# Value projections of four heads in one matmul, and an earlier first quad, in a two-layer encoder trunk

## The chip, the cores and the metric

The kernel runs on one core of a Trainium2 chip. The metric is device time in microseconds (us), the median of several executions of the same program. Beside it stands one execution taken with the hardware profiler, whose rows are quoted here. Its span is the time from the first to the last instruction on the core; the device time of the same execution is a little longer than the span.

Engine names in the profile: PE is TensorE (matmuls), PEld its weight loads, DVE is VectorE, ACT is ScalarE, POOL is GpSimd, and SP issues most of the DMAs. Each engine works through its own instructions in a fixed order; semaphores let one engine wait for another. PSUM, which matmuls write, has eight banks of 128 partitions by 512 fp32 values.

## What is computed

The reference is a streaming encoder trunk on one sequence of 512 tokens, width 1024, two layers, all in fp32. Each layer is:

```python
h = h + 0.5 * swiglu(rmsnorm(h, ffn1_norm), ffn1_w_gu, ffn1_w_down)        # width 2816
u = rmsnorm(h, mix_norm)
b_g, c_g, v_c, q_c, kv_c, k_r, g_conv, g_mla = split(u @ w_in)
y_conv = (b_g * causal_conv3(c_g * v_c)) @ w_conv_out
y_mla = mla(q_c, kv_c, k_r) @ w_mla_out                                     # 8 heads
h = h + (sigmoid(g_conv) * y_conv + sigmoid(g_mla) * y_mla) @ w_o
h = h + 0.5 * swiglu(rmsnorm(h, ffn2_norm), ffn2_w_gu, ffn2_w_down)
h = h + sigmoid(rmsnorm(h, ple_norm) @ w_ple_gate) * (p @ w_ple_proj)
```

The attention (mla) has eight heads with a key and query part of 128 columns, a rotary part of 64 and a value of 128. Keys and values come from a normed latent of width 256 (kv_c), queries from one of width 384 (q_c). The mask lets a token see its own chunk of 64 tokens and all chunks before. A final RMSNorm follows the last layer.

## The kernel before

**Numbers as pairs.** To reach fp32 accuracy, every matmul operand is split into a high part rounded to fp32r and a low part, the rest. A product is three matmuls: high times high, high times low, low times high (`mm3`, L264 to L270). ACT makes a high part by a cast (L260), DVE the low part by a subtraction (L261). Most matmuls have 512 columns, one PSUM bank.

**Weights.** `Stream` brings weights in halves of eight 128x128 tiles (128x1024, 512 KB), in the order in which the kernel asks for tiles. A half is loaded into one of ten raw buffers (L52, queue SP), then split: a cast on ACT (L71, `wh`), a subtraction on DVE (L72, `wl`). There are four buffers for split halves (`N_WH`), and `get` hands out the tiles of the current half one after the other; a request must lie within one half. `fill` tells how many tiles of the current half are used up. During the attention three of the raw buffers hold the turned probabilities (`pt`).

**Buffers of activations.** 44 buffers of 128x512 (`G`) hold all that is not a weight; `gates` (16), the split latent `kvc` (4), keys, queries, values, exponentials and rotary parts share them in the attention.

**PSUM.** `Banks` has two layouts. `paired` has two double banks (`PB`), one double bank (`PA`, for sums that are seeded by a copy) and two single banks (`PS`). `eight` has eight single ones, used in turn; a tile waits until the last reader of the bank's earlier content is done.

**Order.** A planner that knows rough costs puts the instructions of each engine in order when the kernel is built; the earlier an instruction is written, the higher it ranks, but one that can't run yet lets later ones by. The order is then fixed. So the trace, not the source, tells the order on ACT and DVE; TensorE's order follows the source nearly everywhere.

**The first SwiGLU** (`ffn` with `first`, L661 on). Products with the gate and up weights run partly as plain matmuls (`projs`, four columns pairs 0 to 3) and partly as quads: a seven-product scheme over token halves (`Halved`, `Sevens`). A quad needs sums and differences of rows of the input. `Halved.row(j)` is `own(j)`, one multiplication on ACT and one difference on DVE, which give what products 1 and 5 need, and `other(j)`, all the rest, for products 2, 3, 4, 6 and 7. `step(n, 1)` does product 1 into a double bank `b` and has ACT copy it to the seeded double bank `a` (`seed`, L543); `step(n, 2)` goes on adding to `a`. `activate(f)` turns the plain products of column pair f into activations, and `down` multiplies these with the down weights.

**The attention** (`mixer`, from L845). Heads go in four pairs. For a pair, `keys_queries` does key 0, query 0, key 1, query 1 (two and three weight tiles each), `values` the values of both heads. Value weights are fetched by `value_weights` after both queries or between, whichever fits into halves of eight tiles. In `values` the split latent of 128 tokens is the stationary operand, and the weights of the two heads, 256 columns, are the moving one. Two token blocks fill one bank: 24 matmuls of 256 columns and two banks for each pair. `scores` (L925 on) does four score tiles per head, 256 to 512 columns, five matmuls each, and for each a reduction on DVE (L943) and an exponential on ACT (L945). `turn` transposes the probabilities (L955) and splits them into `pt`; `mix_v` multiplies them with the values (L966 to L968).

For pair 0 keys and queries are done in the `paired` layout: key 0 in the first half of `PA`, query 0 in `PB`, key 1 and query 1 in the single banks. Then come `banks.eight()`, the values of pair 0, the table load for the exponential (L987) and the last of eight `conv_out`. The round of pair `pr` does the keys and queries of the next pair with the turning of this pair's first head between, `mix_v` of head 0, the next pair's first scores, its values, the turning of head 1, the next pair's second scores, the rotary part of the pair after that, and `mix_v` of head 1.

Names in the trace: `m0h1v` is layer 0, pair 1, values; `kn`, `qn` and `qr` are keys, queries and rotary queries; `m0s11p` the scores of pair 1, head 1; `m0t01t` the turned tiles of pair 0, head 1; `m0cop` conv_out; `a02b` and `a02a` the double banks of quad 2 of the first SwiGLU.

Of the kernel before, what the change touches and what calls it, by code (L numbers as in the profile page):

```python
# [16 lines left out]
P = 128  # L17
CHUNK = 64
N_HEADS = 8
NOPE = 128  # L20
ROPE = 64
VD = 128
# [160 lines left out]
def trunk_kernel(ctx, tc, dims, x, p, positions, gains, rope_c, final_row, weights, out):  # L183
# [46 lines left out]
    def PS(name):  # L230
        return banks.single.tile([P, 512], F32, tag="mm", name=name)
# [47 lines left out]
    def projs(cols_, vs, pss, part_by_part=False):  # L279

        for k, (vh, vl) in enumerate(vs):
            ws = [W.get(tiles[k]) for tiles in cols_]
            if k == 0 and part_by_part:
                for ps, (wh, _) in zip(pss, ws):
                    nc.tensor.matmul(ps, wh, vh, start=True, stop=False)
                for ps, (_, wl) in zip(pss, ws):
                    nc.tensor.matmul(ps, wl, vh, start=False, stop=False)
                for ps, (wh, _) in zip(pss, ws):
                    nc.tensor.matmul(ps, wh, vl, start=False, stop=False)
                continue  # L290
# [288 lines left out]
    def ffn(l, nm, name, first=False, beside=iter(()), early=2):  # L579
# [85 lines left out]
        if first:  # L665
            pss[0], pss[1] = whole(0), whole(1)
            projs(cs[0] + cs[1], xs, pss[0] + pss[1], True)
            r = norm()
            ys.row(0, xs)
            ys.row(1, xs)  # L670
            activate(0)
            pss[2] = [PS(f"{name}p{w}2") for w in "gu"]
            projs(cs[2], xs, pss[2])
            ys.row(2, xs)
            activate(1)
            ys.row(3, xs)
            pss[3] = whole(3)
            projs(cs[3], xs, pss[3])
            activate(2)
            step(n0, 1)  # L680
            activate(3)
            downs.extend((m, 0) for m in range(KD))
            for j in (2, 6, 5, 7, 3):
                if j in (2, 6, 5):
                    fill()
                step(n0, j)
        else:
            pss[0] = whole(0)
# [12 lines left out]
            step(n0, 7)  # L701
            step(n0, 3)
# [32 lines left out]
    def mixer(l):  # L735
# [108 lines left out]
        class Pair:  # L844
            def __init__(self, pr):  # L845
                self.n = f"{name}h{pr}"
                self.heads = (2 * pr, 2 * pr + 1)
                self.turned, self.q2, self.kn, self.qn, self.v = None, {}, {}, {}, None

            def q_rope(self):  # L850
                ps = proj(W.col("w_uq", l, tuple(hd * (NOPE + ROPE) + NOPE for hd in self.heads), QL), qc, self.n + "qr")
# [14 lines left out]
                ps = proj(W.col("w_uq", l, self.heads[t] * (NOPE + ROPE), QL), qc, f"{self.n}qn{t}", ps)  # L866
                self.qn[t] = split(ps, f"{self.n}qn{t}")

            def value_weights(self):
                self.vw = [W.get(*(("w_ukv", l, k * P, hd * 256 + NOPE) for hd in self.heads)) for k in range(KL // P)]  # L870

            def values(self):
                vs = []
                for tb in range(0, NT, 2):
                    ps = PS(f"{self.n}v{tb}")
                    for b in range(2):
                        tok = slice((tb + b) * P, (tb + b + 1) * P)
                        o = ps[:, b * 256:(b + 1) * 256]
                        for k, (vh, vl) in enumerate(self.vw):
                            ch, cl = kvc[k][0][:, tok], kvc[k][1][:, tok]  # L880
                            nc.tensor.matmul(o, ch, vh, start=k == 0, stop=False)
                            nc.tensor.matmul(o, ch, vl, start=False, stop=False)
                            nc.tensor.matmul(o, cl, vh, start=False, stop=k == len(self.vw) - 1)
                    vs.append(ps)
                self.v = [split(ps, f"{self.n}v{2 * i}") for i, ps in enumerate(vs)]

            def keys_queries(self, turned=None, pss=(None, None)):

                last = W.pairs_fit(2, 10)
                for t in range(2):  # L890
                    self.key(t, None if t else pss[0])
                    if t:
                        self.q_parts()
                        if not last:
                            self.value_weights()
                    self.query(t, None if t else pss[1])
                    if t == 0 and turned:
                        turned()
                if last:
                    self.value_weights()  # L900

        pairs = [Pair(pr) for pr in range(N_HEADS // 2)]
        n_last = KD // 2 - 1
# [55 lines left out]
        def mix_v(pr, t, qk):  # L959
            n = f"{name}o{pr}{t}"  # L960
            ps = PS(n + "av")
            for j in range(NT):
                vh, vl = qk.v[j // 2]
                c = (j % 2) * 256 + t * VD
# [15 lines left out]
        pt_h, pt_l = turned_tiles(name)  # L980
        heads = []
        NP = N_HEADS // 2
        pairs[0].keys_queries(pss=(PA(name + "kn")[:, 0, :], PB(name + "qn")[:, 0, :]))
        banks.eight()
        pairs[0].values()

        nc.scalar.activation(warm, m_b[KD - 1][:, 0:1], AF.Exp)  # L987
        conv_out(KD - 1)
        es = [scores(0, 0, pairs[0])]
        pairs[1].q_rope()  # L990
        es.append(scores(0, 1, pairs[0]))
        for pr in range(NP):
            qk = pairs[pr]
            if pr + 1 < NP:
                nxt, es_n = pairs[pr + 1], []
                nxt.keys_queries(lambda: turn(pr, 0, es[0]))
                heads.append(mix_v(pr, 0, qk))
                es_n.append(scores(pr + 1, 0, nxt))
                nxt.values()
                turn(pr, 1, es[1])  # L1000
                es_n.append(scores(pr + 1, 1, nxt))
                if pr + 2 < NP:
                    pairs[pr + 2].q_rope()
                heads.append(mix_v(pr, 1, qk))
                es = es_n
            else:
                for t in range(2):
                    turn(pr, t, es[t])
                    mla_part(t, 0, N_HEADS - 2)
                    heads.append(mix_v(pr, t, qk))  # L1010
# [261 lines left out]
```

## Time and profile before

| | |
|---|---|
| device time, median of 3 (lowest to highest) | 2266.15 us (2266.03 to 2266.27) |
| device time of the profiled execution | 2266.17 us |
| its span | 2264.0 us |
| granted TensorE clock, mean | 0.999 |
| matmuls | 12176 |
| instructions on DVE, ACT | 2423, 2220 |
| read from memory | 218.94 MB, 98 GB/s over the span |
| DMA queue of the weights | 29.1% of 16 engines' time |

In the waits, "PE x <- DVE y: 1.6, 1, 1.6" is TensorE's instruction on x waiting for DVE's on y: total, times and longest, in us. In the timelines a row has start, duration, engine, line, operation, output and inputs, shape and count; square brackets give idle time before it and what ended it. Matmuls overlap, so the difference of two starts is what one costs. A row of the windows view has the stretch, its length, and the busy time and count of PE, PEld, DVE, ACT and POOL, then the granted clock, the DMA share and GB/s.

### The profile page before, as it was taken

The page shows a single profiled execution, that of the slowest core. Times are in us where ns is not written, and L with a number is a line of the kernel's source. Part 1 is how long each engine was busy: PE and PEld are TensorE (multiplying, and loading weights), DVE is VectorE, ACT ScalarE, POOL GpSimd, SP SyncE. Part 2 cuts the span into 40 slices and gives each one's busy share as a digit, 9 for nine tenths or more (in the row PEclk, how much of TensorE's full clock was granted, in tenths as well). Part 3 has the DMA queues.
Part 4 walks back from the last instruction along what each step waited for, and adds up shares of the span by engine and source line. Part 5 has one row for each costly group of instructions (what it writes and reads, how often), then busy time and mean ns, then how long its engine had stood idle before and what let it go on. Part 6 is the DMA issues. An engine that isn't in the chain of part 4 may idle for free.

```text
span 2264.0 us, 31169 instructions
## 1 busy us (share of the span) xinstructions
PE 2247.3 (99%) x12176; PEld 1953.1 (86%) x12176; DVE 1721.0 (76%) x2423; ACT 1432.2 (63%) x2220; POOL 40.3 (2%) x42
## 2 busy tenths in 40 slices
PE   9999999999999999999999999999999999999998
PEld 7888888888888888888888888888888888888887
DVE  8887767877876877776798777668878678777756
ACT  7666666556744666666676666655567457666664
POOL 0000000000200000000000000000001000000000
PEclk9999999999999999999999999999999999999999
DMA  5232333222122233333222333332222223233321
GB/s 215 98 105 101 112 121 102 70 99 95 50 99 85 85 102 103 103 112 132 83 94 97 102 108 105 112 103 80 98 75 65 103 75 103 97 108 104 111 93 38
DMA packets 63362, 223.04 MB, mean 99 GB/s; under 512 B 7280, under 2 KB 7280, under 8 KB 63216
## 3 DMA queue, kind: packets, MB, share of 16 engines
q1 hardware_dynamic: 62640, 220.28, 29.1%
q8 instruction: 95, 1.56, 0.3%
q10 hardware_dynamic: 576, 0.79, 0.1%
q14 instruction: 51, 0.42, 0.1%
HBM read 218.94 MB, written 2.10 MB: 98 GB/s over the span
## 4 chain that ended last, share of the span: by engine, by line
PE 98%; DVE 1%; ACT 1%; issue 0%; DMA 0%; SPq 0%; DVEq 0%; ACTq 0%
PE a1pd L268 2%; PE b1pd L268 2%; PE b0pd L268 2%; PE a0pd L268 2%; PE b1pd L269 2%; PE a1pd L269 2%; PE b0pd L269 2%; PE a1pd L270 2%; PE b0pd L270 2%; PE b1pd L270 2%; PE a0pd L269 2%; PE a0pd L270 2%; PE m0mop L268 1%; PE m1mop L269 1%; PE m0mop L269 1%; PE m1mop L270 1%
## 5 line engine op out<-in xcount | busy, mean ns | idle before, releaser
L72 DVE TENSOR_TENSOR wl<-st,wh 128x1024 fp32r<-128x1024 f32 (+1 forms) x504 | 610.3, 1213 | 322.2 <-ACT wh L71 321.3
L71 ACT CAST wh<-st 128x1024 fp32r<-128x1024 f32 (+1 forms) x503 | 523.7, 1044 | 420.9 <-issue 13.6
L152 DVE TENSOR_TENSOR st<-st,st 128x1024 f32<-128x1024 f32 x47 | 57.5, 1224 | 1.3
L72 DVE TENSOR_TENSOR wl<-s,wh 128x1024 fp32r<-128x1024 f32 x47 | 57.3, 1219 | 0.6 <-ACT wh L71 0.4
L154 DVE TENSOR_TENSOR s<-st,st 128x1024 f32<-128x1024 f32 x47 | 57.3, 1219 | 0.2
L149 DVE TENSOR_TENSOR st<-st,s 128x1024 f32<-128x1024 f32 x47 | 57.3, 1218 | 0.0
L157 DVE TENSOR_TENSOR st<-st,st 128x1024 f32<-128x1024 f32 x47 | 57.2, 1217 | 0.0
L71 ACT CAST wh<-s 128x1024 fp32r<-128x1024 f32 x47 | 49.0, 1042 | 8.8 <-PE a1p L269 2.6
L632 ACT ACTIVATE h<-a0pd 128x512 f32<-128x512 f32 x40 | 23.7, 596 | 17.7 <-PE a0pd L270 17.5
L632 ACT ACTIVATE h<-b1pd 128x512 f32<-128x512 f32 x40 | 23.7, 596 | 16.8 <-PE b1pd L270 16.7
L632 ACT ACTIVATE h<-b0pd 128x512 f32<-128x512 f32 x40 | 23.7, 596 | 16.8 <-PE b0pd L270 16.6
L632 ACT ACTIVATE h<-a1pd 128x512 f32<-128x512 f32 x40 | 23.7, 596 | 16.4 <-PE a1pd L270 16.3
L628 ACT ACTIVATE a0pd<-h 128x512 f32<-128x512 f32 x40 | 24.0, 602 | 2.5 <-DVE a010o L548 1.7
L628 ACT ACTIVATE b1pd<-h 128x512 f32<-128x512 f32 x40 | 24.0, 603 | 2.2 <-DVE b110o L548 1.4
L628 ACT ACTIVATE a1pd<-h 128x512 f32<-128x512 f32 x40 | 24.0, 602 | 2.2 <-DVE a110o L548 1.4
L628 ACT ACTIVATE b0pd<-h 128x512 f32<-128x512 f32 x40 | 24.0, 603 | 2.2 <-DVE b010o L548 1.4
L107 POOL MEMSET wh<- 128x256 f32 x4 | 1.1, 314 | 1180.0 <-DVE wl L72 1180.0
L270 PE MATMUL a0p<-a0x,wl 128*128 128x512 f32 x44 | 17.1, 389 | 0.0
L268 PE MATMUL a0p<-a0x,wh 128*128 128x512 f32 x44 | 17.1, 389 | 0.0
L269 PE MATMUL a0p<-a0x,wh 128*128 128x512 f32 x44 | 17.1, 389 | 0.0
L263 ACT ACTIVATE b0x<-h,cols 128x512 fp32r<-128x512 f32 x8 | 5.8, 725 | 13.3 <-DVE h L1022 13.3
L263 ACT ACTIVATE b1x<-h,cols 128x512 fp32r<-128x512 f32 x8 | 5.8, 723 | 13.3 <-DVE h L1022 13.3
(6663 smaller groups left out, 7534.7 us busy)
## 6 DMA issues: line engine op xcount, KB each, us to landing
st<-in_weights SPq DMA_DIRECT2D x406, 512.0 KB, 3.3
h<-in_x SPq DMA_DIRECT2D x8, 256.0 KB, 5.5
st<-in_weights SPq DMA_DIRECT2D x7, 256.0 KB, 5.4
out<-e1d SPq DMA_DIRECT2D x4, 256.0 KB, 2.1
out<-fh SPq DMA_DIRECT2D x3, 256.0 KB, 2.2
e0pi<-in_p SPq DMA_DIRECT2D x2, 256.0 KB, 3.7
e1pi<-in_p SPq DMA_DIRECT2D x2, 256.0 KB, 3.5
fg<-in_final_row SPq DMA_DIRECT2D x2, 256.0 KB, 4.1
```

The source lines that it names most:

```text
L71: self.nc.scalar.copy(hi[:, w], src[:, w])
L72: self.nc.vector.tensor_tensor(lo[:, w], src[:, w], hi[:, w].bitcast(F32), ALU.subtract)
L149: tt(self.a12, self.a12, self.s, ALU.subtract)
L152: tt(self.a11, self.a11, self.a21, ALU.subtract)
L154: tt(self.s, self.a22, self.a11, ALU.subtract)
L157: tt(self.a21, self.a21, self.a22, ALU.add)
L263: nc.scalar.activation(hi, src, AF.Copy, scale=scale)
L268: nc.tensor.matmul(ps, wh, vh, start=first, stop=False, skip_group_check=seeded)
L269: nc.tensor.matmul(ps, wh, vl, start=False, stop=False, skip_group_check=seeded)
L270: nc.tensor.matmul(ps, wl, vh, start=False, stop=last, skip_group_check=seeded)
L628: nc.scalar.mul(ps, h[m], 2.0)
L632: nc.scalar.mul(h[m], ps, 0.5)
```

## The change

In the attention, the values of two pairs (four heads) are now done together for pairs 0 and 1 and for pairs 2 and 3: the weights of four heads make 512 columns, one bank per block of 128 tokens, 24 matmuls and four banks for two pairs. The value weights are fetched at the first place in `keys_queries` of the even pair where four or eight tiles of the current half are used up. The values of pairs 0 and 1 are done after the last `conv_out`, which is now written ahead of them; those of pairs 2 and 3 at the end of the round of pair 1. For pair 0 the second query goes to the second half of `PA` in place of a single bank.

In the first SwiGLU, row 3 is cut into its two parts: `own(3)` stays, and `other(3)` comes after product 1 of the first quad, which itself moves ahead of `activate(2)`.

```diff
             ys.row(2, xs)
             activate(1)
-            ys.row(3, xs)
+            ys.own(3, xs)
             pss[3] = whole(3)
             projs(cs[3], xs, pss[3])
+            step(n0, 1)
+            ys.other(3, xs)
             activate(2)
-            step(n0, 1)
             activate(3)
...
-            def value_weights(self):
-                self.vw = [W.get(*(("w_ukv", l, k * P, hd * 256 + NOPE) for hd in self.heads)) for k in range(KL // P)]
-
-            def values(self):
-                vs = []
-                for tb in range(0, NT, 2):
-                    ps = PS(f"{self.n}v{tb}")
-                    for b in range(2):
-                        tok = slice((tb + b) * P, (tb + b + 1) * P)
-                        o = ps[:, b * 256:(b + 1) * 256]
-                        for k, (vh, vl) in enumerate(self.vw):
-                            ch, cl = kvc[k][0][:, tok], kvc[k][1][:, tok]
-                            nc.tensor.matmul(o, ch, vh, start=k == 0, stop=False)
-                            nc.tensor.matmul(o, ch, vl, start=False, stop=False)
-                            nc.tensor.matmul(o, cl, vh, start=False, stop=k == len(self.vw) - 1)
-                    vs.append(ps)
-                self.v = [split(ps, f"{self.n}v{2 * i}") for i, ps in enumerate(vs)]
-
-            def keys_queries(self, turned=None, pss=(None, None)):
-
-                last = W.pairs_fit(2, 10)
+            def value_weights(self, nxt):
+
+                if nxt and self.vw is None and W.fill() % 4 == 0:
+                    hds = self.heads + nxt.heads
+                    self.vw = [W.get(*(("w_ukv", l, k * P, hd * 256 + NOPE) for hd in hds)) for k in range(KL // P)]
+
+            def values(self, tb, nxt):
+
+                ps = PS(f"{self.n}v{tb}")
+                tok = slice(tb * P, (tb + 1) * P)
+                for k, (vh, vl) in enumerate(self.vw):
+                    ch, cl = kvc[k][0][:, tok], kvc[k][1][:, tok]
+                    nc.tensor.matmul(ps, ch, vh, start=k == 0, stop=False)
+                    nc.tensor.matmul(ps, ch, vl, start=False, stop=False)
+                    nc.tensor.matmul(ps, cl, vh, start=False, stop=k == len(self.vw) - 1)
+                v = split(ps, f"{self.n}v{tb}")
+                self.v.append((v, 0))
+                nxt.v.append((v, 2 * VD))
+
+            def keys_queries(self, nxt=None, turned=None, pss=((None, None), (None, None))):
+
                 for t in range(2):
-                    self.key(t, None if t else pss[0])
+                    self.value_weights(nxt)
+                    self.key(t, pss[0][t])
                     if t:
                         self.q_parts()
-                        if not last:
-                            self.value_weights()
-                    self.query(t, None if t else pss[1])
+                    self.value_weights(nxt)
+                    self.query(t, pss[1][t])
                     if t == 0 and turned:
                         turned()
-                if last:
-                    self.value_weights()
+                self.value_weights(nxt)
...
-        pairs[0].keys_queries(pss=(PA(name + "kn")[:, 0, :], PB(name + "qn")[:, 0, :]))
+        pk, pq = halves(PA(name + "kn"))
+        pairs[0].keys_queries(pairs[1], pss=((pk, None), (PB(name + "qn")[:, 0, :], pq)))
         banks.eight()
-        pairs[0].values()
+        conv_out(KD - 1)
+        for tb in range(NT):
+            pairs[0].values(tb, pairs[1])
 
         nc.scalar.activation(warm, m_b[KD - 1][:, 0:1], AF.Exp)
-        conv_out(KD - 1)
...
-                nxt.keys_queries(lambda: turn(pr, 0, es[0]))
+                after = pairs[pr + 2] if pr % 2 and pr + 2 < NP else None
+                nxt.keys_queries(after, lambda: turn(pr, 0, es[0]))
                 heads.append(mix_v(pr, 0, qk))
                 es_n.append(scores(pr + 1, 0, nxt))
-                nxt.values()
                 turn(pr, 1, es[1])
                 es_n.append(scores(pr + 1, 1, nxt))
                 if pr + 2 < NP:
                     pairs[pr + 2].q_rope()
                 heads.append(mix_v(pr, 1, qk))
+                for tb in range(NT if after else 0):
+                    nxt.values(tb, after)
```

`mix_v` now takes the tile and the first column of each token block from the list that `values` fills.

More of the change, by code (lines that the diff above doesn't have):

```diff
@@ L847, in __init__ @@
                 self.heads = (2 * pr, 2 * pr + 1)
-                self.turned, self.q2, self.kn, self.qn, self.v = None, {}, {}, {}, None
+                self.turned, self.q2, self.kn, self.qn, self.v, self.vw = None, {}, {}, {}, [], None
             def q_rope(self):
@@ L897, in keys_queries @@
                     if t == 0 and turned:
                         turned()
-                if last:
-                    self.value_weights()
+                self.value_weights(nxt)
+                assert self.vw or not nxt
         pairs = [Pair(pr) for pr in range(N_HEADS // 2)]
@@ L962, in mix_v @@
             for j in range(NT):
-                vh, vl = qk.v[j // 2]
-                c = (j % 2) * 256 + t * VD
+                (vh, vl), c = qk.v[j]
+                c += t * VD
                 o = ps[:, S - pt_h[j].shape[1]:]
```

## The prediction

> **What bounds the kernel now.** I read the page first, then the list of who waited for whom on TensorE, then the timeline of each engine around the places that the change touches.
>
> ```profile
> span 2264.0 us, 31169 instructions
> PE 2247.3 (99%) x12176; PEld 1953.1 (86%) x12176; DVE 1721.0 (76%) x2423; ACT 1432.2 (63%) x2220; POOL 40.3 (2%) x42
> PE 98%; DVE 1%; ACT 1%; issue 0%; DMA 0%; SPq 0%; DVEq 0%; ACTq 0%
> ```
>
> TensorE is busy for 2247.3 of 2264.0 us, and 98% of the chain that ends last is its own matmuls. So an edit is worth something only if it makes TensorE's stream shorter or takes away one of its waits, and the waits are few:
>
> ```profile
> PE a02a L525 <- ACT a02a L543: 1.7, 1, 1.7
> PE m0h0v L881 <- DVE m0h0qn1l L261: 1.6, 1, 1.6
> PE m1h0v L881 <- DVE m1h0qn1l L261: 1.6, 1, 1.6
> PE a02d L538 <- ACT a02d L543: 1.2, 1, 1.2
> ...
> PE m0s11p L936 <- ACT m0s10e L945: 0.6, 1, 0.6
> PE m1s11p L936 <- ACT m1s10e L945: 0.6, 1, 0.6
> ```
>
> The change aims at three of the six places: the values of pair 0 in both layers (m0h0v, m1h0v) and the first quad of the first SwiGLU (a02a). It also moves work past a fourth and fifth, the scores of pair 1 (s11p). All six together are 8.3 us, 0.4% of the time, so this is a change of a few tenths of a per cent at most. The profiled execution took 2266.17 us, 2.2 more than its span, and the median of the three runs is 2266.15; the sum below is made against 2266.17. A measurement of this kernel can tell about 0.2%, 4.5 us, from no change.
>
> **Values as 512 columns.** Before, each of four pairs and two layers has 24 matmuls of 256 columns (L881 to L883): 192. After, two pairs share 24 of 512 columns: 96. The columns streamed are the same, so only the fixed part of a matmul is saved. The timeline of TensorE gives starts of both kinds:
>
> ```profile
> 552.70 0.39 PE L268 MATMUL m0h0kn<-m0kvn0h,wh 128*128 128x512 f32 x1
> ...
> 555.87 0.39 PE L270 MATMUL m0h0qn<-m0qn,wl 128*128 128x512 f32 x1
> 556.10 0.28 PE L881 MATMUL m0h0v<-wh,m0kvn0h 128*128 128x256 f32 x1
> ...
> 557.41 0.28 PE L883 MATMUL m0h0v<-wh,m0kvn1l 128*128 128x256 f32 x1
> 559.26 0.39 PE L881 MATMUL m0h0v<-wh,m0kvn0h 128*128 128x256 f32 x1 [1.57 <-DVE m0h0qn1l L261]
> ...
> 560.80 0.40 PE L268 MATMUL m0cop<-m0yc0h,wh 128*128 128x512 f32 x1
> ...
> 563.32 0.39 PE L270 MATMUL m0cop<-m0yc3h,wl 128*128 128x512 f32 x1
> 563.54 0.28 PE L936 MATMUL m0s00p<-m0h0kn0h,m0h0qn0h 128*128 128x256 f32 x1
> ...
> 566.76 0.40 PE L268 MATMUL m0h1qr<-m0qn,wh 128*128 128x512 f32 x1
> ```
>
> The durations overlap (0.39 and 0.28 us), so starts count. Eleven steps of 256 columns take 557.41 - 556.10 = 1.31 us, 0.1191 each. Fourteen steps of 512 columns take 3.17 us, 0.2264 each; eleven more in the row's second group take 2.52, 0.2291 each. Two of the first against one of the second save 0.0091 to 0.0118 us, times 96: 0.9 to 1.1 us. I take **-1.0**.
>
> The Trainium skill (TensorE: Matmul & The Clock Gate, section "Wait — 56ns, not 53.3ns?") says that start to start is the columns over 2.4 GHz plus about 2.5 ns for each matmul. By that rule, an estimate from that page, 96 matmuls fewer would save 0.24 us and the whole sum would end 0.8 us higher. The trace does not agree on the size of the fixed part: both of its steps lie 0.010 to 0.013 us above that rule, so the measured saving decides.
>
> **The bank wait goes.** In each layer TensorE stands between 557.41 and 559.26: 1.85 us for a step of 0.12, so 1.73 are lost, 3.46 in two layers. The row that ends it:
>
> ```profile
> 558.51 0.69 DVE L261 TENSOR_TENSOR m0h0qn1l<-m0h0qn,m0h0qn1h 128x512 fp32r<-128x512 f32 x1
> ```
>
> The second tile of values has been given the bank of the second query, and that query is read until 559.20. After the change this query lies in the second half of the seeded pair of banks (pq) and the first key in the first half; and the last conv_out, 563.54 - 560.80 = 2.74 us of matmuls, is issued ahead of the values. From 556.10 on TensorE would do conv_out to 558.84, then four tiles of six 512-column matmuls, 1.37 each: 560.21, 561.58, 562.95, 564.32. A bank that comes free at 559.20 holds up only its first or second tile: 3.1 us if conv_out got it, 0.4 if the first tile of values did, nothing later. In the trace the first two tiles after the switch to eight banks got the two single banks, and the second query is no longer in one. I take no wait: **-3.46**, with +6.2 and 0 as the ends. Moving conv_out itself costs TensorE nothing; its product (L806) is wanted only at the end of the mixer. The evictions are eight splits per layer either way. The exponential's table load, 1.28 us on ACT, stays before the scores, which start 0.8 us later than now.
>
> **The cover that is lost.** The values of pairs 1, 2 and 3, 2.88 us each (585.14 to 588.02 in the rows below), stand between the scores of one head and the turning of another. While TensorE does them, DVE and ACT reduce and exponentiate. Now pairs 0 and 1 are done together in front of the scores of pair 0, and pairs 2 and 3 at the end of pair 1's round. In the rounds from there the next head's scores come 2.88 us sooner after the last, on the same eight banks: without value tiles, score tile i gets the bank of score tile i of the head before (four turned tiles lie between).
>
> ```profile
> 585.14 0.28 PE L881 MATMUL m0h1v<-wh,m0kvn0h 128*128 128x256 f32 x1
> ...
> 588.02 1.25 PE L955 MATMUL m0t01t<-ident,m0s01e 128*128 128x128 f32 x10
> 589.03 0.36 PE L936 MATMUL m0s11p<-m0h1kn1h,m0h1qn1h 128*128 128x256 f32 x1
> ...
> 589.58 0.28 PE L940 MATMUL m0s11p<-m0kr,m0h1qr 128*128 128x256 f32 x1
> 590.51 0.39 PE L936 MATMUL m0s11p<-m0h1kn1h,m0h1qn1h 128*128 128x256 f32 x1 [0.64 <-ACT m0s10e L945]
> ...
> 592.08 0.39 PE L936 MATMUL m0s11p<-m0h1kn1h,m0h1qn1h 128*128 128x512 f32 x1
> ```
>
> ```profile
> 582.10 1.22 DVE L72 TENSOR_TENSOR wl<-st,wh 128x1024 fp32r<-128x1024 f32 x1
> ...
> 584.95 1.21 DVE L72 TENSOR_TENSOR wl<-st,wh 128x1024 fp32r<-128x1024 f32 x1
> ...
> 586.98 1.20 DVE L72 TENSOR_TENSOR wl<-st,wh 128x1024 fp32r<-128x1024 f32 x1
> ...
> 588.16 0.66 DVE L943 TENSOR_REDUCE m0s10sm<-m0s10p 128x1 f32<-128x512 f32 x1
> ```
>
> ```profile
> 580.80 2.00 ACT L71 CAST wh<-st 128x1024 fp32r<-128x1024 f32 x2
> ...
> 589.66 0.70 ACT L945 ACTIVATE m0s10e<-m0s10p,m0s10sm 128x512 f32<-128x512 f32 x1
> ```
>
> Pair 1 already waits here: 590.51 - 589.58 - 0.12 = 0.81 us, for the last exponential of s10, ended 590.36. After, the fourth tile of s11 takes the bank of that last tile of s10, and TensorE is there 2.88 + 0.81 sooner than now: 592.08 - 3.69 = 588.4. With the order of ACT and DVE as it is, it waits until 590.4, 2.0 us. But the first of the three weight splits (582.10, 1.22 us) has to move, since its half is due sooner (rival c), and the two value splits leave. If DVE's stretch moves up by 1.22, the last reduction ends near 587.6, the exponential near 588.5, and the wait is 0 to 0.4. I take 0.4 in place of 0.81: **-0.8** in two layers; the ends are -1.6 (gone) and +2.4 (2.0 each).
>
> Pairs 2 and 3 have no wait now. In pair 3's round the turned tile follows the last exponential closely:
>
> ```profile
> 637.48 1.25 PE L955 MATMUL m0t21t<-ident,m0s21e 128*128 128x128 f32 x10
> ```
>
> ```profile
> 636.92 0.69 ACT L945 ACTIVATE m0s30e<-m0s30p,m0s30sm 128x512 f32<-128x512 f32 x1 [0.49 <-DVE m0s30sm L946]
> ...
> 638.17 0.59 ACT L260 CAST m0pt<-m0t21t 128x512 fp32r<-128x512 f32 x1
> ```
>
> mix_v stands behind the turning (1.0 us, 588.02 to 589.03 above) and the scores s31 (3.2: s00 has the same shapes, 563.54 to 566.76) and needs that tile. TensorE now comes to it at 637.48 + 4.2 = 641.7, and then at 638.8. The cast, without the value cast ahead of it, ends near 638.2 and DVE's half of the split 0.6 to 0.9 later. I cost 0.3 per layer, **+0.6**, with 0 and 1.2 as the ends.
>
> **The first quad.** `step(n0, 1)` and its seed copy (L543) are issued ahead of the second half of row 3 and of activate(2).
>
> ```profile
> 51.94 1.11 PE L529 MATMUL a02b<-a0x,wl 128*128 128x256 f32 x8
> 53.13 0.61 ACT L260 CAST a0t3h<-a0t 128x512 fp32r<-128x512 f32 x1
> 53.65 1.00 ACT L543 COPY a02a<-a02b 128x1024 f32<-128x1024 f32 x1
> 54.71 2.14 PE L525 MATMUL a02a<-a0x,wh 128*128 128x512 f32 x8 [1.66 <-ACT a02a L543]
> ```
>
> The quad's products end at 53.05 (51.94 + 1.11), the copy takes 1.00, and ahead of it on ACT stands the cast of row 3, begun at 53.13. With the two changed over, the copy ends at 54.13 and gains 0.5; the other 1.1 of the wait is the copy itself, and nothing else is ready for TensorE. The cast then is 1.0 later, and so are row 3's sums, which step 6 needs. ACT's order was planned before either was ready, so it may stay. I take **-0.3**, with -1.66 (other matmuls fill the wait) and +1.0 as the ends. The later wait for a02d has the same make-up and stays.
>
> **Sum:** -1.0 - 3.46 - 0.8 + 0.6 - 0.3 = -4.96; 2266.17 - 4.96 = **2261.2 us**.
>
> **The rivals.** (a) *All waits close*: pair 1's goes, a02a's is filled, pairs 2 and 3 lose nothing: -1.0 - 3.46 - 1.6 - 1.66 = -7.7, 2258.5. For it: DVE is then lighter in that stretch. Against: the copy's own 1.0 us.
>
> (b) *The cover is missed*: pair 1 waits 2.0, pairs 2 and 3 0.6 per layer, a02a is unchanged: -1.0 - 3.46 + 2.4 + 1.2 = -0.9, 2265.3. For it: three splits of 1.2 us lie among the reductions now. Against: the first must move.
>
> (c) *Weights late, slower than before*:
>
> ```profile
> 578.63 0.39 PE L268 MATMUL m0h1qn<-m0qn,wh 128*128 128x512 f32 x1
> ```
>
> ```profile
> 556.10:576.48 20.38, 18.81 (x112) 16.65 (x110) 14.16 (x38) 11.28 (x28) 3.90 (x4) 1.00 0.09 27
> ```
>
> The ring holds four split halves of eight weight tiles. The value weights of two pairs now fill the end of one half and the start of the next, and both stay until the fourth value tile, 564.3, where the older came free near 556 before. The half after the next two is first needed, by my count of tiles, at the second tile of pair 1's second query (578.63 in the old frame; its third matmul, which reads the low half, near 579.1), not at its values. Its cast and subtraction stand at 580.80 and 582.10 now, the latter ended at 583.32. If they stay there TensorE stands 4.2 us per layer, and pair 1's later wait goes: -1.0 - 3.46 - 1.6 + 0.6 - 0.3 + 8.4 = +2.6, 2268.8. It outweighs the gains from 2.9 us per layer on, and makes the kernel slower by over 0.2% from 5.2. For it: this half is cast late although a buffer was free by my count. Against: in the window before (556.10 to 576.48) DVE is busy for 14.16 and ACT for 11.28 of 20.38 us, so there is room, and every other half is cast long before its use.
>
> (d) *The change doesn't do what it says*: a value tile or conv_out still gets a bank that is read late, and 1.7 us per layer come back: 2264.7.
>
> **How the numbers follow.** Forecast 0.45, (a) 0.17, (b) 0.15, (c) 0.13, (d) 0.10. Two thirds of the forecast's own spread lies below 2261.6, so faster by over 0.2%: 0.30 + 0.17 + 0.03 from (d)'s and (b)'s milder forms = 0.50. Slower by over 0.2%, above 2270.7: 0.06 from (c)'s longer forms, 0.02 from conv_out's bank. The rest, 0.42, is within 0.2%. The range, 2257.5 to 2267.5, reaches past (a), (b) and (d) and cuts most of (c).
>
> **What would show it.** In the changed profile: no wait of m0h0v and m1h0v on a query's split; steps of 0.226 to 0.230 between the 512-column values; scores of pair 0 starting 8.2 us after the second query ends, not 7.4; a wait of s11p of 0 to 0.4 per layer; a02a still over 1.0. A wait of the second query of pair 1 on a weight split would prove (c) and the forecast wrong; more than 1.5 us on s11p per layer, (b).

## The result, and the profile after

The changed kernel takes 2260.81 us (median of 11 executions, 2260.25 to 2261.25), the kernel before 2266.27 in the same comparison (2265.97 to 2266.82). The ratio is 0.9976, 95% interval 0.9966 to 0.9985: 5.5 us less, just beyond what can be told from no change. The profiled execution took 2260.81 us too. Its page, the lines on the span and the engines:

```profile
span 2258.7 us, 30986 instructions
PE 2246.9 (99%) x12080; PEld 1947.6 (86%) x12080; DVE 1719.7 (76%) x2423; ACT 1432.2 (63%) x2220; POOL 37.3 (2%) x42
```

There are 96 matmuls fewer, and the other engines have the same number of instructions. The list of TensorE's waits is now three lines long:

```profile
PE a02a L525 <- ACT a02a L543: 1.7, 1, 1.7
PE a02d L538 <- ACT a02d L543: 1.2, 1, 1.2
PE idle L376 <- DVE hpi L305: 1.0, 1, 1.0
```

The waits of the values (m0h0v, m1h0v) and of pair 1's scores (s11p) are gone, all four. That of the first quad (a02a), at which one half of the change aimed, stands as it did. TensorE's timeline around the first values of layer 0:

```profile
556.58 0.39 PE L268 MATMUL m0cop<-m0yc0h,wh 128*128 128x512 f32 x1
...
559.07 0.39 PE L270 MATMUL m0cop<-m0yc3h,wl 128*128 128x512 f32 x1
559.30 0.39 PE L882 MATMUL m0h0v<-wh,m0kvn0h 128*128 128x512 f32 x1
...
564.51 0.39 PE L884 MATMUL m0h0v<-wh,m0kvn1l 128*128 128x512 f32 x1
564.74 0.28 PE L937 MATMUL m0s00p<-m0h0kn0h,m0h0qn0h 128*128 128x256 f32 x1
```

From conv_out to the scores no step is longer than the others: 24 values in 564.74 - 559.30 = 5.44 us, 0.2267 each. For the rounds of pairs 1, 2 and 3, the windows of after, each from a pair's first key to the next pair's (the last to the output product), and then those of before:

```profile
577.67:599.39 21.72, 21.72 (x126) 19.03 (x125) 21.45 (x53) 18.75 (x42) 6.25 (x5) 1.00 0.29 92
599.39:626.35 26.96, 26.96 (x151) 23.62 (x149) 23.20 (x56) 18.73 (x44) 3.92 (x4) 1.00 0.12 43
626.35:642.28 15.93, 15.93 (x102) 14.59 (x100) 14.23 (x42) 10.98 (x30) 3.46 (x4) 1.00 0.21 70
```

```profile
576.48:601.66 25.18, 24.54 (x150) 22.02 (x149) 22.25 (x54) 19.98 (x44) 5.32 (x5) 1.00 0.26 84
601.66:625.94 24.28, 24.28 (x151) 21.98 (x149) 21.33 (x54) 17.65 (x42) 5.49 (x4) 1.00 0.13 44
625.94:644.74 18.80, 18.80 (x126) 17.51 (x125) 16.75 (x45) 12.18 (x32) 3.98 (x4) 1.00 0.17 58
```

The rounds differ by -3.46, +2.68 and -2.87. The stretch of pair 0, from its second key (552.70 before, 552.93 after) to the first of these rounds, went from 23.78 to 24.74, +0.96. The sum is -2.69, and layer 1 gives the same: -5.38 for both layers, which is the whole result.

Two things are new. The second query of pair 0 starts late. All engines' timeline of after:

```profile
552.93 0.39 PE L268 MATMUL m0h0kn<-m0kvn0h,wh 128*128 128x512 f32 x1
...
553.67 0.68 DVE L261 TENSOR_TENSOR m0h0kn0l<-m0kn,m0h0kn0h 128x512 fp32r<-128x512 f32 x1
...
554.06 0.39 PE L270 MATMUL m0h0kn<-m0kvn1h,wl 128*128 128x512 f32 x1
...
554.40 0.19 PEld L268 LDWEIGHTS m0kn<-m0qn,wh 128*128 128x128 f32 x1 [0.37 <-DVE m0h0kn0l L261]
554.40 0.50 PE L268 MATMUL m0kn<-m0qn,wh 128*128 128x512 f32 x1
...
554.74 0.39 PE L269 MATMUL m0kn<-m0qn,wh 128*128 128x512 f32 x1
```

The query is written to the second half of the double bank `m0kn`. DVE still subtracts the first key, in its first half, until 554.35, and the row names that subtraction as what ended the wait. Two steps take 0.34 in place of 0.23: one for the wait, one for the start after it. That is 0.22 us per layer.

And the second query of pair 1 is cut in pieces (TensorE's timeline of after):

```profile
579.60 0.39 PE L270 MATMUL m0h1qn<-m0qn,wl 128*128 128x512 f32 x1
579.82 0.39 PE L967 MATMUL m0o00av<-m0pt,m0h0v0h 128*128 128x512 f32 x1
...
582.71 0.40 PE L268 MATMUL m0h1qn<-m0qn,wh 128*128 128x512 f32 x1
...
583.18 0.28 PE L940 MATMUL m0s10p<-m0kr,m0h1qr 128*128 128x256 f32 x1
...
583.76 0.34 PE L939 MATMUL m0s10p<-m0h1kn0h,m0h1qn0l 128*128 128x384 f32 x1
584.09 0.50 PE L270 MATMUL m0h1qn<-m0qn,wl 128*128 128x512 f32 x1
...
589.81 0.39 PE L937 MATMUL m0s11p<-m0h1kn1h,m0h1qn1h 128*128 128x512 f32 x1
```

After three of its nine matmuls TensorE goes on with the values' product and the first scores, and does the rest among them. The reason is on ACT and DVE, one timeline each:

```profile
575.74 0.58 ACT L946 ACTIVATE m0s01e<-m0s01p,m0s01sm 128x384 f32<-128x384 f32 x1 [2.24 <-DVE m0s01sm L944]
...
579.88 1.26 ACT L859 CAST m0h1qr<-m0h1qrt 64x512 fp32r<-64x512 f32 x2
581.17 1.05 ACT L71 CAST wh<-st 128x1024 fp32r<-128x1024 f32 x1
...
588.63 0.71 ACT L946 ACTIVATE m0s10e<-m0s10p,m0s10sm 128x512 f32<-128x512 f32 x1
```

```profile
582.81 1.23 DVE L72 TENSOR_TENSOR wl<-st,wh 128x1024 fp32r<-128x1024 f32 x1
...
587.69 0.67 DVE L944 TENSOR_REDUCE m0s10sm<-m0s10p 128x1 f32<-128x512 f32 x1
```

The weight half of the query's later tiles is cast at 581.17 and subtracted until 584.04, as late as rival (c) of the prediction feared. But the planner knew it and put other matmuls in front, so the 4.2 us of standing did not come. The step from 583.76 to 584.09 is long (0.33 for 0.17), and so is the one behind it (0.33 for 0.23). From the place of the cut to the turned tile TensorE takes 586.61 - 579.82 = 6.79 us; before, the same matmuls took 585.14 - 578.63 = 6.51. So the cut costs 0.28 us per layer.

### The profile page after: what moved, and what is told of

It is laid out like the page before. It is cut to its first block, busy times and chain, and to the rows that moved or that the text cites. A ratio compares the mean times of both kernels' runs of the same rounds, so it can differ in the third digit from the quotient of the medians.

```text
span 2258.7 us, 30986 instructions
## 1 busy us (share of the span) xinstructions
PE 2246.9 (99%) x12080; PEld 1947.6 (86%) x12080; DVE 1719.7 (76%) x2423; ACT 1432.2 (63%) x2220; POOL 37.3 (2%) x42
## 4 chain that ended last, share of the span: by engine, by line
PE 99%; ACT 0%; DVE 0%; issue 0%; DVEq 0%; ACTq 0%
PE b1pd L268 2%; PE b0pd L268 2%; PE a1pd L268 2%; PE a0pd L268 2%; PE a1pd L269 2%; PE b0pd L269 2%; PE b1pd L269 2%; PE b1pd L270 2%; PE a1pd L270 2%; PE b0pd L270 2%; PE a0pd L269 2%; PE a0pd L270 2%; PE m0mop L268 1%; PE m0mop L269 1%; PE m1mop L268 1%; PE m1mop L270 1%
```

## Experiments

The theory to be tested is the prediction's account with the trace's sizes. Each part gives what its terms say, and the parts add. The rivals are named in each expectation.

**The two halves of the change, each alone.** First the changed kernel with the first SwiGLU as before:

```diff
-            ys.own(3, xs)
+            ys.row(3, xs)
             pss[3] = whole(3)
             projs(cs[3], xs, pss[3])
-            step(n0, 1)
-            ys.other(3, xs)
             activate(2)
+            step(n0, 1)
             activate(3)
```

> The attention part of the change alone; the first SwiGLU as before. Theory A (all of the 5.5 us comes from the attention, since the changed kernel still waits 1.7 us for a02a as before): 2260.8 us, within 0.4 of the whole change. Rival B (the moved quad gives some of it elsewhere, by the order of ACT and DVE): 2261.5 or more.

Measured: 2261.08 us (2260.45 to 2261.51), ratio 0.9976 (0.9966 to 0.9985). Then the kernel before with only the edit of the first SwiGLU, the reverse of this diff:

> The first SwiGLU part of the change alone; the attention as before. Theory A: 2266.2 us, no different from before, and the same wait of 1.7 us for a02a. Rival B: 2265.5 or less, or a shorter wait.

Measured: 2266.60 (2265.81 to 2266.86), ratio 1.0000 (0.9991 to 1.0009), and the wait of a02a is 1.7 in its profile as before. All of the gain is the attention's; the moved quad does nothing.

**The attention's two parts, each alone.** The kernel before with the new banks and conv_out ahead of the values, but narrow values for each pair (the cut lines let `keys_queries` take a bank for each key and query):

```diff
...
-        pairs[0].keys_queries(pss=(PA(name + "kn")[:, 0, :], PB(name + "qn")[:, 0, :]))
+        pk, pq = halves(PA(name + "kn"))
+        pairs[0].keys_queries(pss=((pk, None), (PB(name + "qn")[:, 0, :], pq)))
         banks.eight()
+        conv_out(KD - 1)
         pairs[0].values()
 
         nc.scalar.activation(warm, m_b[KD - 1][:, 0:1], AF.Exp)
-        conv_out(KD - 1)
```

> Before with the second query in the second half of the seeded double bank and the last conv_out ahead of the values; values stay narrow, 256 columns, pair by pair. Theory A (the wait of pair 0's values is the bank of the second query and nothing else): the wait of 1.73 us goes in both layers, the second query starts 0.23 us later in each (it shares a double bank with the first key, whose low half is read until then), so -3.5 + 0.5 = -3.0 us, 2263.2; the wait of s11p stays at 0.8. Rival B (the wide values themselves remove the wait, by later demand): the wait stays at least in part, 2264.5 or more.

Measured: 2263.38 (2262.69 to 2263.66), ratio 0.9985 (0.9977 to 0.9994), 3.2 less than before. TensorE's waits in its profile, the last two lines:

```profile
PE m0s11p L936 <- ACT m0s10e L945: 0.6, 1, 0.6
PE m1s11p L936 <- ACT m1s10e L945: 0.6, 1, 0.6
```

The values no longer wait, the scores of pair 1 still do, and the second query starts 0.34 after the key's last matmul, as after. The other way round, the changed kernel with the second query of pair 0 in a single bank and conv_out behind the values:

```diff
-        pk, pq = halves(PA(name + "kn"))
-        pairs[0].keys_queries(pairs[1], pss=((pk, None), (PB(name + "qn")[:, 0, :], pq)))
+        pairs[0].keys_queries(pairs[1], pss=((PA(name + "kn")[:, 0, :], None), (PB(name + "qn")[:, 0, :], None)))
         banks.eight()
-        conv_out(KD - 1)
         for tb in range(NT):
             pairs[0].values(tb, pairs[1])
 
         nc.scalar.activation(warm, m_b[KD - 1][:, 0:1], AF.Exp)
+        conv_out(KD - 1)
```

> The changed kernel with key and query 1 of pair 0 back in single banks and the last conv_out behind the values. Theory A: the second of four wide value tiles gets the second query's bank; it is asked for 1.37 us after the query's end, 557.5, and free at 559.2, so 1.7 us wait in each layer come back, less 0.23 for the query: 2260.8 + 3.0 = 2263.8. Rival B: the wait doesn't come back, 2260.4.

Measured: 2264.33 (2263.74 to 2264.70), ratio 0.9990 (0.9981 to 0.9999), 2.2 less than before. Its waits:

```profile
PE m0h0v L882 <- DVE m0h0qn1l L261: 1.6, 1, 1.6
PE m1h0v L882 <- DVE m1h0qn1l L261: 1.6, 1, 1.6
```

The bank wait is back, the scores of pair 1 do not wait, the query of pair 0 starts on time. The two parts give 3.2 and 2.2, together 5.4; the change gives 5.5. So the two parts add up. The second query's bank and the earlier conv_out were not tried apart, so how much of the first part each gives is not shown.

**The cover of the scores.** The banks alone, with the narrow values of the next pair moved from between its scores to the end of the round. The cover goes, but no value is shared (the lines that this edit has in common with the banks alone are left out):

```diff
                 es_n.append(scores(pr + 1, 0, nxt))
-                nxt.values()
                 turn(pr, 1, es[1])
...
                 heads.append(mix_v(pr, 1, qk))
+                nxt.values()
                 es = es_n
```

> Banks as changed, values narrow and pair by pair, but at the end of each round, so that nothing stands between the scores of one head and the turning of the other. Theory A (pair 1's wait is the chain of the last reduction and exponential of s10 behind weight splits; taking the values' 2.88 us of cover away makes it longer, and the changed kernel escaped because its planner put most of the late second query among the scores): s11p waits 1 to 2 us in each layer, 2263.8 to 2265.8. Rival B (the wait goes as soon as the value splits leave the stretch): no wait, 2263.4 - 1.8 = 2261.6.

Measured: 2262.27 (2261.78 to 2262.82), ratio 0.9981 (0.9972 to 0.9990). The waits of s11p in its profile:

```profile
PE m1s11p L936 <- ACT m1s10e L945: 0.3, 1, 0.3
PE m0s11p L936 <- ACT m0s10e L945: 0.3, 1, 0.3
```

By starts TensorE stands 0.44 there, against 0.80 with the cover. Neither side had it: the wait falls by half though 2.88 us of matmuls that covered it are gone. With the cover, these rows of DVE and ACT stood ahead of the last reduction of s10 and of its exponential (the banks alone, one timeline each):

```profile
585.70 1.20 DVE L72 TENSOR_TENSOR wl<-st,wh 128x1024 fp32r<-128x1024 f32 x1
```

```profile
586.58 1.05 ACT L71 CAST wh<-st 128x1024 fp32r<-128x1024 f32 x1 [0.47 <-PE m0h1v L883]
```

They split weights, not values: the value splits came behind the exponential in that kernel too (from 589.06). With the values at the end of the round, the next such subtraction stands at 591.93 and the next such cast at 595.84. What waits has changed too: with the cover it was the second tile of s11, for the last exponential of s10; now it is the third tile, for the third exponential, and the fourth starts at 587.97, before the last exponential ends at 588.45. What of this outweighs the lost cover, no run separates. The second query of pair 1 is whole here. Its trace shows one new stand of 0.12 in the scores of pair 3 (s31p), with 0.11 for the start after it. From the second key of pair 0 to the output product, the two layers are 0.3 us shorter than with the banks alone; the medians say 1.1, and where the rest comes from is open.

**Why the weight half is late.** First a fifth buffer for split halves, paid for with two raw buffers:

```diff
-N_RAW = 10
-N_WH = 4
+N_RAW = 8
+N_WH = 5
```

> The changed kernel with five buffers of split halves and eight raw ones in place of four and ten. Theory C (the second query of pair 1 is cut up because the two halves that hold the value weights leave the ring too few): its nine matmuls stand together again and the 0.3 us of broken steps per layer go, 2260.2; if the cut-up query was what covered the exponentials of s10 (theory A), s11p waits again, 0.5 to 2 us per layer, 2261 to 2264. Rival B: the query whole and no wait, 2260.2. Rival D (the half is late for another reason than the ring): the query stays cut up, 2260.8.

Measured: 2263.20 (2262.23 to 2264.76), ratio 0.9986 (0.9978 to 0.9995). The query is cut at the same place, and the long step is still there (584.21 to 584.53). So a fifth buffer alone doesn't bring the half forward. The time is 2.4 us longer than the change's; the expectation had such a time only with a wait of s11p, and s11p doesn't wait. The profile has two new waits of 0.6 and 0.4 in the first SwiGLU (a0pd), but a02d's of 1.2 is gone, so the listed waits do not make up the 2.4 us. That the missing raw buffers cost them is likely, but not shown. Then the order: the half is split right after pair 1's first key in the code, and handed out later. This is on top of the next experiment, the first key in a single bank:

```diff
+        self.ready = []
...
-        if c == 0:
+        if c == 0 and self.ready:
+            self.tiles, self.hi, self.lo = self.ready.pop(0)
+        elif c == 0:
...
+    def split_next(self):
+
+        tiles = []
+        self.ready.append((tiles, *self.split(self.raw(tiles))))
...
                     self.key(t, pss[0][t])
+                    if t == 0 and self is pairs[1]:
+                        W.split_next()
```

> The kernel with the first key in a single bank (2260.2), and the eight weight tiles that pair 1's second query runs into are cast and subtracted right after that pair's first key in the code, instead of where the second query first asks for them. Theory A (it was only the planned order on ScalarE and VectorE that put this half behind the rope casts, not a slot of the ring): the nine matmuls of that query run without a break, the gap of 0.15 per layer ahead of its later matmuls is gone, s11p still does not wait, 2259.7 to 2260.0. Rival B (the 1.05 and 1.2 us of the earlier cast and subtraction push the exponentials of pair 0 back, and TensorE waits there): a new wait of 0.3 us or more per layer in the scores of pair 0, 2260.6 or more. Rival C (the half is late for a slot, or the cut costs nothing): 2260.2 and the query still cut, or whole without a gain.

Measured: 2259.31 (2259.00 to 2259.94), ratio 0.9969 (0.9958 to 0.9981), the fastest of all. TensorE's timeline of this kernel:

```profile
580.18 0.39 PE L277 MATMUL m0h1qn<-m0qn,wh 128*128 128x512 f32 x1
580.40 0.39 PE L278 MATMUL m0h1qn<-m0qn,wl 128*128 128x512 f32 x1
580.63 0.39 PE L977 MATMUL m0o00av<-m0pt,m0h0v0h 128*128 128x512 f32 x1
```

Its lines are numbered up to ten higher. The nine matmuls run in one piece, and the list of waits has no new one: the planner now casts the half at 563.70, between the value splits of pair 0. So it was the planned order that made it late; neither its data nor a buffer was missing. From pair 1's first key to pair 2's is 598.65 - 577.12 = 21.53 against 21.72, 0.2 per layer: the 0.28 of the cut, less 0.1 that the scores s11p now take longer. Pair 2's round gains 0.1 more. That makes 0.6 of the 0.9 between the medians of this kernel and the one it is built on.

**The late query of pair 0.** The changed kernel with the first key in a single bank, so that the second query alone uses the double bank:

```diff
-        pk, pq = halves(PA(name + "kn"))
-        pairs[0].keys_queries(pairs[1], pss=((pk, None), (PB(name + "qn")[:, 0, :], pq)))
+        pq = PA(name + "qn1")[:, 1, :]
+        pairs[0].keys_queries(pairs[1], pss=((None, None), (PB(name + "qn")[:, 0, :], pq)))
```

> The changed kernel with the first key of pair 0 in a single bank, so that the seeded double bank holds the second query alone. Theory A (the second query of pair 0 starts 0.23 us late because DVE still reads the first key from the other half of the same tile): the two steps of 0.34 at its first matmuls become 0.23, 0.45 us in two layers, 2260.4. Rival B: another cause, unchanged, 2260.8.

Measured: 2260.20 (2259.83 to 2260.71), ratio 0.9973 (0.9962 to 0.9983). All engines' timeline:

```profile
553.83 0.68 DVE L261 TENSOR_TENSOR m0h0kn0l<-m0h0kn,m0h0kn0h 128x512 fp32r<-128x512 f32 x1
...
554.23 0.39 PE L270 MATMUL m0h0kn<-m0kvn1h,wl 128*128 128x512 f32 x1
...
554.46 0.39 PE L268 MATMUL m0qn<-m0qn,wh 128*128 128x512 f32 x1
```

DVE's subtraction stands as it did relative to TensorE, to 554.51, and the query's first matmul starts 0.23 after the last of the key, while the subtraction runs. It is the shared tile that made it wait, not DVE's load.

**The first quad.** The quad's first step was put ahead of the fourth plain products, so that they could cover the copy:

```diff
             ys.own(3, xs)
+            step(n0, 1)
             pss[3] = whole(3)
             projs(cs[3], xs, pss[3])
-            step(n0, 1)
             ys.other(3, xs)
```

> The changed kernel with product 1 of the first quad ahead of the fourth pair's plain products, which are 48 matmuls or 10.9 us. Theory A (the wait for a02a is the seed copy of 1.0 us, with nothing on TensorE to cover it): the wait of 1.8 us goes, 2259.0. Rival B (the weights of the quad or another wait are late in its place): 2260.5 or more.

Measured: 2262.31 (2261.73 to 2262.53), ratio 0.9981 (0.9973 to 0.9990), 1.5 us slower than the change. The planner put the quad's next steps directly behind the first and the plain products behind them (a0p at 50.87; after, the quad's first step stood at 50.36). The waits:

```profile
PE a02a L525 <- ACT a02a L543: 1.7, 1, 1.7
...
PE a0p L268 <- DVE a0un L621: 0.8, 1, 0.8
PE a02b L525 <- DVE a0u L261: 0.4, 1, 0.4
```

Then the third activation was put between the step and row 3's second half, on the kernel with the first key in a single bank, so that the first down products are ready during the copy:

```diff
             step(n0, 1)
-            ys.other(3, xs)
             activate(2)
+            ys.other(3, xs)
             activate(3)
```

> The kernel with the first key in a single bank (2260.2), and in the first SwiGLU the third activation is put between the first quad's first step and the second half of row 3. Theory A (the wait for the seed copy is long because nothing else is ready, and the copy stands behind row 3's cast): with the activation ahead of row 3's second half, the first matmuls of the down projection are ready during the copy, six of them (1.4 us) are done in the wait, and the wait falls from 1.7 to 0.3 or less: 2258.6 to 2259.2. Theory B (what the wait loses is only moved): the sixth step finds row 3's sums later and waits for them, 2259.8 to 2260.5, and a new wait stands on a02b. A wait of a02a still over 1.2 would speak against both.

Measured: 2261.75 as median of ten executions (2260.40 to 2264.11; an eleventh of 5803.06 is left out), ratio 0.9980 (0.9971 to 0.9989). That is 1.5 slower than the kernel it is built on, outside the ranges of both theories. The waits in its profile:

```profile
PE a02d L538 <- ACT a02d L543: 1.9, 1, 1.9
...
PE a0pd L268 <- ACT a0a3h L260: 0.8, 1, 0.8
PE a0pd L269 <- DVE a0a3l L261: 0.6, 1, 0.6
```

The wait of a02a is filled by six down products, as theory A had it. But row 3's sums and the fourth activation come later, and TensorE waits for them and for the second seed copy. From the quad's first matmul to a02d's first it takes 68.81 - 50.82 = 17.99 us, after 67.86 - 50.36 = 17.50, for the same matmuls. So what is taken off one wait appears at the next. That the stretch is short of ACT's and DVE's time is a likely reading, not shown. The other part of the loss is told in the last section. Both edits together:

> Both edits of this call on the kernel with the first key in a single bank (2260.2). If they are independent, the sum of their two differences from 2260.2: by theory A of both 2258.1 to 2259.0. If only the activation's place counts, 2258.6 to 2259.2; if neither, 2260.2.

Measured: 2260.43 (2259.51 to 2262.52), ratio 0.9975 (0.9965 to 0.9985), 1.1 slower than the early half alone. By the medians, the two differences from 2260.20 are -0.9 and +1.5 and would give 2260.9, so the two edits may well be independent. No time of the expectation came out, since each took the activation's place for a gain or for nothing. The executions of the two kernels with it are spread over 3 us and more, those of the kernel with five buffers over 2.5, those of the others over 1 us or so.

## Why the prediction was right, and where not

The forecast was 2261.2 us, the result is 2260.81, and it is faster, the likeliest of the three signs. The sum was -4.96; the profiled execution ends 5.36 sooner. Its terms, in us for the whole kernel:

| term | predicted | by the trace |
|---|---|---|
| values as 512 columns | -1.0 | -1.1 |
| the bank wait | -3.46 | -3.7 |
| the cover lost at pair 1 | -0.8 | -1.8 |
| the cover lost at pairs 2 and 3 | +0.6 | +0.2 |
| the first quad | -0.3 | 0 |
| the second query of pair 0 late | none | +0.4 |
| the second query of pair 1 cut | in rival (c) alone | +0.6 |

The measured column adds up to -5.4, as do the windows of both layers (-5.38). That the sum came so near is in part luck: the first four terms together gave 1.7 us more than was thought, and the last three took 1.3 back, of which 1.0 was in no term of the sum. One figure ahead of the sum is wrong as well: the six waits that the prediction counts are 7.3 us, not 8.3 (8.3 takes in the 1.0 at L376, which the change doesn't touch); no term rests on it. Ahead of the first quad the profiled execution of after is 0.2 later than that of before, as it can be between executions of one kernel.

**512 columns.** A layer's values took 96 steps of 0.1191, 11.43 us, and now take 48 of 0.2267, 10.88; twice 0.55 is 1.1. The prediction weighed a rule of the Trainium skill (TensorE: Matmul & The Clock Gate, section "Wait — 56ns, not 53.3ns?") under which an estimate from that page would have been 0.24. The trace does not agree: the measured steps, not that fixed part, gave the size.

**The bank wait.** The mechanism was right: the wait went with the banks and conv_out alone, and came back without them. Its price was short by what follows a wait: TensorE's first step after it takes 0.10 longer, 0.22 for 256 columns in place of 0.12 (559.26 to 559.48 before). With that the wait was worth 1.83 per layer.

**The cover at pair 1.** The term was mis-sized. The last reduction was thought to end at 587.6 in the old count, 588.8 in that of after, where everything here stands 1.19 later; it ended at 588.36. The exponential ended at 589.34 and TensorE came to the tile at 589.81, so the whole wait went, 0.81 and 0.10 for the start after it. The narrow values at the end of the round left 0.44, what the prediction took. There it is the third tile that waits, for the third exponential, and not the fourth for the last, as the prediction had it. ACT's rows show a difference at that place: with the narrow values, four casts of the turned tile (584.96 to 586.24) stand ahead of the third exponential, which ends at 586.86, when TensorE has been at the tile since 586.56; after, one cast (587.59) stands ahead of it, it ends at 588.67, and TensorE comes to the third tile at 588.89. So the planned order on ACT would account for the last 0.44; no run tests it by itself. It is not the cut query that delays TensorE, since the kernel with the half split early has the query whole and no such wait in its list either.

**Pairs 2 and 3.** The turned tile was never late: its first casts ended at 636.67, its last subtraction at 638.60, and mix_v came at 639.32. The mechanism named for this term did not occur. What is left is 0.1 in pair 2's round, in the scores s21p.

**The first quad.** ACT's order stayed, which the prediction held possible but did not take as its value. ACT's timeline of after:

```profile
53.37 0.61 ACT L260 CAST a0t3h<-a0t 128x512 fp32r<-128x512 f32 x1
53.89 1.00 ACT L543 COPY a02a<-a02b 128x1024 f32<-128x1024 f32 x1
```

Row 3's cast still stands ahead of the seed copy, though the copy's input was there at about 53.3. This move in the source did not change the planned order; why not, the trace can't tell.

**Rival (c)** had the right half and the right lateness, and a wrong price: 8.4 us came out as 0.6. It priced the wait as if TensorE's order were that of the source, as the section on the kernel has it for nearly everywhere; here the planner had let twenty other matmuls by. Rivals (a) and (d) fell with the waits, (b) with the cover.

What the prediction missed altogether is the late second query of pair 0. The diff shows it: two halves of one tile, one still read while the other is written.

## What to carry to other kernels

Where TensorE is busy for 99% of the span, look for the few places where it stands, find for each the reader that holds the bank, and change which tile gets that bank or what is done before: this was worth more (3.2 us with the conv_out moved) than making the matmuls fewer (1.1). Price a late operand by what a planner can put in front of it, not by its lateness; price cover that is lost together with the work that moves away on the other engines. In this kernel two halves of one tile were one thing to whoever waited for it, so give tiles with different last readers to different buffers.

## What the runs showed of the hardware that was not expected

In the profile with the third activation moved, the granted clock fell to half for some time. The windows of that kernel, from 67 us on (the granted clock is the third number from the end):

```profile
67.00:69.00 2.00, 0.19 (x1) 0.20 (x2) 0.42 (x1) 2.00 (x5) 0.00 (x0) 1.00 0.33 131
69.00:70.00 1.00, 1.00 (x8) 0.91 (x8) 0.00 (x0) 1.00 (x2) 0.00 (x0) 1.00 0.00 0
...
71.00:73.00 2.00, 2.00 (x6) 1.51 (x6) 0.50 (x1) 0.00 (x0) 0.00 (x0) 0.50 0.23 66
```

TensorE had stood 0.9, 0.8 and 2.1 us, the last until 68.81, and was busy again for 1.3 us when the clock halved. From 70.26 to 73.61 steps of 512 columns took 0.43 in place of 0.23, some 1.5 us in all. With the early half added, the profile shows the same stands and no such stretch. That kernel's executions of 2259.51 to 2260.43 have a mean clock of 0.999, those of 2261.05 to 2262.52 one of 0.998 or 0.997. Of the other kernels only two have executions below 0.999: the one with the activation moved alone (three of ten) and the one with five buffers (four of eleven, among its five slowest). So stands can cost more than their length, and in some executions only. The Trainium skill (TensorE: Matmul & The Clock Gate, section "What's actually happening") says that the clock halves after an idle window of about 3.4 us, that windows run freely, and that the rate comes back after a busy one. The trace agrees on the half rate (0.50) and on the length of the slow stretch (about 3.4 us). It differs on the cause: no stand here was longer than 2.1 us, and TensorE was busy for 1.3 of the 3.4 us before the drop. How much of a window must be busy, no run here shows.
